# Norms by column group between products, earlier first weights, and another place for a convolution

## The chip, the cores and the metric

One core of a Trainium2 chip. The metric is the device time of one execution in microseconds, the median of the runs shown. Matrix products run on TensorE (PE); VectorE (DVE), ScalarE (ACT) and GpSimd (POOL) do the elementwise work; SyncE (SP) issues most of the other transfers, ScalarE those of the weights.

## The reference

One inference step of a two-layer decoder trunk, width 1024, on 1024 prompt tokens and 64 sample tokens (8 sequences of 8). All is float32. Cut to what matters here:

```python
def rmsnorm(x, g):
    y = x * lax.rsqrt(jnp.mean(x * x, axis=-1, keepdims=True) + NORM_EPS)
    return y * g

# layer 0: short gated convolution and RWKV-7 recurrence side by side
z = rmsnorm(x, norm_mix[0]) @ w_in0
x = x + concat(short_conv(z[:, :1536]), rwkv7(z[:, 1536:])) @ w_out0
x = x + swiglu(rmsnorm(x, norm_ffn[0]), w_gate[0], w_up[0], w_down[0])
# layer 1: forgetting attention (with a paged cache) and Mamba-2 side by side
z = rmsnorm(x, norm_mix[1]) @ w_in1
x = x + concat(attention(...), mamba2(...)) @ w_out1
x = x + swiglu(rmsnorm(x, norm_ffn[1]), ...)
y = rmsnorm(x, norm_final)
```

The FFN's hidden width is 2816. Beside y the step returns new convolution, shift, recurrence and cache rows.

## The kernel before

Activations lie transposed: 1024 features in eight tiles of 128 partitions, tokens along the columns. The 1088 tokens are worked on in two halves. H0 has 576 columns (64 sample, 512 prompt), taken as groups of 320 and 256 columns; H1 has the other 512 prompt columns, taken as one group. In the last layer's output projection and FFN the halves are cut anew: F0 has 512 columns, F1 576.

Each float32 product is three products of two rounded parts (`mm3`, L203 to L206): high by high, low by high, high by low. A weight tile of 128 output features is eight such triples for each column group, 24 matmuls, into one PSUM bank (four banks are named `acc`). `load_w` (L192) fetches the tile in 512 KB on ScalarE's queue, ScalarE rounds it to `wh`, and `k.low` subtracts to get `wl`: POOL, except in the third stage, where it is VectorE. The buffers of `wraw`, `wh` and `wl` are two deep, so a tile's rounding waits until the tile before the last has been used.

A norm (`rms`, L227, and `rms_split`) squares the eight tiles on ScalarE (L237), sums them on VectorE (L239), adds over partitions by matmuls with ones (L245), scales (L247) and takes the power -1/2 on POOL (L224), broadcasts the result over the partitions by matmuls (L255), and multiplies the eight tiles on VectorE (L269); `split` (L216) rounds each on ScalarE (L218) and subtracts on VectorE and POOL in turn (L219). All columns of a half go through each step together, and the products that follow need all of it.

The order of work is the order in which Python generators are stepped. `weave(dense, side, rate)` steps the side chain `rate` times for each step of the dense one; `beside(gen, other)` steps both in turn; `drain` runs one to its end. Each engine runs its own instructions in that order.

Layer 0: norm of H0; projection of H0 for the recurrence, with the norm of H1 woven in; then the first recurrence (of H0) beside H0's short convolution, H1's projection and three steps of H1's short convolution; then the recurrence of H1 beside H0's output projection and FFN (`out_ffn`), with six more steps of the convolution as `fill` in its norm. The last three steps stand beside the mixer norm of H0 for layer 1. A step of the convolution is one weight tile. The third stage runs H1's FFN, mixer norm and `dense` and then F0's projection and FFN beside attention and Mamba-2 of both halves. F1 comes last, with no side work, but for the final norm of F0 beside a part of it.

## Time and profile before

| | |
|---|---|
| median of 3 runs | 3342.81 us (3340.84 to 3344.05) |
| the profiled execution | 3342.04 us, span 3340.3 us |
| mean granted TensorE clock | 0.974 |
| busy share of the span | PE 95%, DVE 57%, ACT 32%, POOL 25% |

A matmul's duration in the trace is longer than the distance between two of them, since they overlap; the distance between starts is what a product costs in a row of products. The granted clock has two levels; a stretch's clock is its mean.

### The profile page before, as it was taken

Reading aid. Unit: us, or ns where it says so; the run is one execution under the profiler, and the core shown is the slowest. Engines: PE = TensorE matmul, PEld = TensorE weight load, DVE = VectorE, ACT = ScalarE, POOL = GpSimd, SP = SyncE. Lnnn points to the kernel's source line nnn. Section 1 sums busy time; section 2 is a strip of 40 time slices with the busy share of each in tenths; the row PEclk is TensorE's granted clock in tenths of the full one; section 3 lists DMA queues with packets and bytes.
Section 4 is the critical chain, followed back from the end, with each engine's and each line's share of the span. In section 5 each row is a group of like instructions: output and inputs, shape, how many; then the busy total and the mean of one; then the engine's idle time right before and its main releaser. Section 6 shows DMA issues by size and latency. Waiting matters only on the chain. (4 is left out here: it accounts for less than half of the span.)

```text
span 3340.3 us, 63263 instructions
## 1 busy us (share of the span) xinstructions
PE 3169.4 (95%) x25213; PEld 2666.9 (80%) x25213; DVE 1906.4 (57%) x3643; ACT 1058.7 (32%) x2083; POOL 834.7 (25%) x561
## 2 busy tenths in 40 slices
...
GB/s 178 116 59 79 87 96 118 73 59 56 51 66 83 83 108 148 191 151 135 108 135 163 199 154 213 240 221 175 172 171 138 113 110 135 87 105 81 83 83 78
DMA packets 238471, 409.20 MB, mean 123 GB/s; under 512 B 37632, under 2 KB 129664, under 8 KB 238176
## 3 DMA queue, kind: packets, MB, share of 16 engines
...
## 5 line engine op out<-in xcount | busy, mean ns | idle before, releaser
L204 PE MATMUL acc<-hh,wh 128*128 128x320 f32 (+2 forms) x3720 | 1264.9, 341 | 17.6 <-ACT hh L218 14.7
L206 PE MATMUL acc<-hh,wl 128*128 128x320 f32 (+2 forms) x3720 | 1255.4, 338 | 7.4 <-POOL wl L198 6.5
L205 PE MATMUL acc<-hl,wh 128*128 128x320 f32 (+2 forms) x3720 | 1254.8, 338 | 7.2 <-DVE hl L219 5.4
L204 PEld LDWEIGHTS acc<-hh,wh 128*128 128x128 f32 x3720 | 712.3, 192 | 97.5 <-ACT hh L218 19.4
L198 POOL TENSOR_TENSOR wl<-wraw,wh 128x1024 fp32r<-128x1024 f32 x225 | 539.6, 2398 | 1000.6 <-ACT wh L196 924.7
L196 ACT CAST wh<-wraw 128x1024 fp32r<-128x1024 f32 (+1 forms) x398 | 416.0, 1045 | 1139.4 <-PE acc L205 1054.1
L206 PEld LDWEIGHTS acc<-hh,wl 128*128 128x128 f32 x3720 | 712.8, 192 | 74.7 <-issue 11.1
L205 PEld LDWEIGHTS acc<-hl,wh 128*128 128x128 f32 x3720 | 713.0, 192 | 72.1 <-DVE hl L219 9.1
L205 PE MATMUL acc<-hidl,wh 128*128 128x320 f32 (+2 forms) x1056 | 353.1, 335 | 0.6 <-DVE hidl L219 0.6
L893 DVE TENSOR_TENSOR x<-x,acc 128x320 f32<-128x320 f32 (+2 forms) x528 | 270.3, 527 | 139.1 <-PE acc L206 136.1
L206 PE MATMUL acc<-hidh,wl 128*128 128x320 f32 (+2 forms) x1056 | 349.5, 332 | 0.0
L204 PE MATMUL acc<-hidh,wh 128*128 128x320 f32 (+2 forms) x1056 | 348.9, 337 | 0.4 <-ACT hidh L218 0.4
L198 DVE TENSOR_TENSOR wl<-wraw,wh 128x1024 fp32r<-128x1024 f32 x173 | 210.9, 1219 | 145.3 <-ACT wh L196 143.2
L1297 POOL DMA_INDIRECT kv<-in_cv,vidx x64 | 75.5, 1180 | 628.8 <-DVE kt L1249 134.4
L204 PEld LDWEIGHTS acc<-hidh,wh 128*128 128x128 f32 x1056 | 198.7, 189 | 24.0 <-issue 4.2
L205 PEld LDWEIGHTS acc<-hidl,wh 128*128 128x128 f32 x1056 | 199.2, 189 | 19.1 <-issue 2.2
L206 PEld LDWEIGHTS acc<-hidh,wl 128*128 128x128 f32 x1056 | 199.5, 189 | 15.6 <-issue 1.4
L219 DVE TENSOR_TENSOR hidl<-ft,hidh 128x512 fp32r<-128x512 f32 (+2 forms) x148 | 178.7, 1207 | 55.9 <-ACT hidh L218 55.8
L881 DVE SCALAR_TENSOR_TENSOR ft<-ft,acc 128x320 f32<-128x320 f32 (+2 forms) x132 | 70.1, 531 | 213.1 <-PE acc L206 212.9
L875 DVE SCALAR_TENSOR_TENSOR ft<-ft,acc 128x320 f32<-128x320 f32 (+2 forms) x132 | 69.7, 528 | 177.0 <-ACT ft L874 176.8
L218 ACT CAST hidh<-ft 128x512 fp32r<-128x512 f32 (+2 forms) x148 | 75.1, 507 | 117.5 <-DVE ft L881 114.3
L1249 DVE STREAM_TRANSPOSE kt<-kv 128x1024 f32<-128x1024 f32 x64 | 79.3, 1239 | 33.8 <-DMA kv<-in_ck 29.9
...
## 6 DMA issues: line engine op xcount, KB each, us to landing
wraw<-in_wi ACTq DMA_DIRECT2D x100, 512.0 KB
...
kv<-in_ck SPq DMA_DIRECT2D x512, 64.0 KB
...
```

Of the source, the lines that this page charges most:

```text
L196: nc.scalar.copy(wh, raw)
L198: k.low.tensor_sub(wl, raw, wh)
L204: mm(acc, wh, xh, start=first, stop=False)
L205: mm(acc, wh, xl, start=False, stop=False)
L206: mm(acc, wl, xh, start=False, stop=last)
L218: k.nc.scalar.copy(hh, v)
L219: (eng or k.nc.vector).tensor_sub(hl, v, hh)
L875: nc.vector.scalar_tensor_tensor(s[:, a:b], s[:, a:b], 1.0, pc, op0=ALU.add, op1=ALU.mult)
L881: nc.vector.scalar_tensor_tensor(s[:, a:b], s[:, a:b], 0.5, pu, op0=ALU.mult, op1=ALU.mult)
L893: nc.vector.tensor_add(xs[n][:, a:b], xs[n][:, a:b], acc[:, :b - a])
L1249: V.transpose(kt, kr)
L1297: nc.gpsimd.indirect_dma_start(out=v, out_offset=None, in_=A["cv"].rearrange("o (s r) c -> (o s) (r c)", r=2), in_offset=bass.IndirectOffs ...
```

## The change

`rms_split` becomes a class `Norm`. `group(a, b)` makes the norm of one column group; `pair` makes group 0, then the first weight tile times group 0 (below p0g0), then the norm of group 1, then the other three products of the first two weight tiles (p1g0, p0g1, p1g1). It is used before the first projection of H0, all four FFNs, and both `dense`; the norm of H1 in layer 0 is one group of 512 columns. H1 and F0 get `two`, halves of 256 columns, where a norm needs two groups. Inside `rms` the power and the broadcasts are now in one step.

In `out_ffn` the last two output tiles are made for group 0 and then for group 1, and the last down products of an FFN go by group, with both weight tiles loaded ahead. All twelve steps of H1's short convolution are now in `first()`, and the rate there is 4.2. At the start the first two weights are fetched before x, which comes in two column groups; part of the constants is loaded by `ready()`, inside the norm of H1.

```diff
 QY = 2
 VY = 3
-
-CF = (3, 6)
 
 
 class Half:
...
         self.g0 = segs[0][1] * (NS + HP) + segs[0][2]
 
...
@@ -237,7 +242,7 @@
         nc.scalar.activation(sq, x[:, lo:hi], AF.Square)
         if i:
             nc.vector.tensor_add(ss, ss, sq)
-        if i % 2:
+        if i % 4 == 3:
             yield
     pt = k.bank(tag)
     nb = len(blocks)
@@ -246,31 +251,43 @@
     r = k.bp.tile([P, 16], F32, name="rs", tag="rs", bufs=2)
     nc.vector.tensor_scalar(r[:, 8:8 + nb], pt[:, :nb], 1.0 / width, EPS, op0=ALU.mult, op1=ALU.add)
     rsqrt(k, r[:, 0:nb], r[:, 8:8 + nb])
-    yield
     out = []
     for a, b in groups:
         pb = k.bank(tag)
         for j, (_, c, w) in enumerate(blocks):
             if a <= c < b:
-                nc.tensor.matmul(pb[:, c - a:c - a + w], r[:, j:j + 1].to_broadcast([P, P]), k.con("ident")[:, :w], start=True, stop=True)
+                nc.tensor.transpose(pb[:, c - a:c - a + P], r[:, j:j + 1].to_broadcast([P, P]), k.con("ident"))
         out.append((a, b, pb[:, :b - a]))
     yield
     return out
 
 
-def rms_split(k, H, xs, gname):
-
-    nc = k.nc
-    h = k.parts(H)
-    rs = yield from rms(k, H, xs, D)
-    for i in range(KT):
-        v = k.ft(H)
-        for a, b, r in rs:
-            nc.vector.scalar_tensor_tensor(v[:, a:b], xs[i][:, a:b], k.col(gname, i), r, op0=ALU.mult, op1=ALU.mult)
-        split(k, h[0][i], h[1][i], v, nc.gpsimd if i % 2 else nc.vector)
-        if i % 2:
-            yield
-    return h
+class Norm:
+
+
+    def __init__(self, k, H, xs, gname):
+        self.k, self.H, self.xs, self.gname = k, H, xs, gname
+        self.h = k.parts(H)
+
+    def group(self, a, b):
+        k, h = self.k, self.h
+        (_, _, r), = yield from rms(k, self.H, self.xs, D, [(a, b)])
+        for i in range(KT):
+            v = k.ft(self.H)[:, a:b]
+            k.nc.vector.scalar_tensor_tensor(v, self.xs[i][:, a:b], k.col(self.gname, i), r, op0=ALU.mult, op1=ALU.mult)
+            split(k, h[0][i][:, a:b], h[1][i][:, a:b], v, k.nc.gpsimd if i % 2 else k.nc.vector)
+            if i % 4 == 3:
+                yield
+
+    def pair(self, w0, w1, m0=P, m1=P):
+
+        k, h = self.k, self.h
+        (a, b), (c, d) = self.H.two
+        yield from self.group(a, b)
+        p0 = gemm_tile(k, w0, h, a, b, m0)
+        yield from self.group(c, d)
+        p1 = gemm_tile(k, w1, h, a, b, m1)
+        return [p0, gemm_tile(k, w0, h, c, d, m0)], [p1, gemm_tile(k, w1, h, c, d, m1)]
 
 
 def by8(ap):
...
@@ -853,31 +875,39 @@
         split(k, y[0][i], y[1][i], v)
         if i % 4 == 3:
             yield
-    xs = []
-    for n in range(KT):
-        w = load_w(k, A["wo%d" % l][n])
-        x = k.xt(H)
-        for a, b, h, c, g in H.pieces(0, H.W):
-            nc.sync.dma_start(x[:, a:b], k.xs[h][n][:, c:c + b - a] if l else A["xT"][n][:, g:g + b - a])
-        for a, b in H.groups:
-            nc.vector.tensor_add(x[:, a:b], x[:, a:b], gemm_tile(k, w, y, a, b))
-        xs.append(x)
-        yield
-    h = yield from beside(rms_split(k, H, xs, "nf%d" % l), fill)
+    xs, ws = [], []
+
+    for n, js in [(n, (0, 1)) for n in range(KT - 2)] + [(n, (j,)) for j in range(2) for n in (KT - 2, KT - 1)]:
+        if not js[0]:
+            ws.append(load_w(k, A["wo%d" % l][n]))
+            x = k.xt(H)
+            for a, b, h, c, g in H.pieces(0, H.W):
+                nc.sync.dma_start(x[:, a:b], k.xs[h][n][:, c:c + b - a] if l else A["xT"][n][:, g:g + b - a])
+            xs.append(x)
+        for a, b in (H.two if len(js) > 1 else H.two[js[0]:js[0] + 1]):
+            nc.vector.tensor_add(xs[n][:, a:b], xs[n][:, a:b], gemm_tile(k, ws[n], y, a, b))
+        if len(js) > 1 or n == KT - 1:
+            yield
+    nr = Norm(k, H, xs, "nf%d" % l)
+    h = nr.h
+    first = yield from nr.pair(load_w(k, A["wg%d" % l][0]), load_w(k, A["wu%d" % l][0]))
...
@@ -893,13 +923,17 @@
                     nc.vector.tensor_add(xs[n][:, a:b], xs[n][:, a:b], acc[:, :b - a])
                     yield
 
-        if last and g == NF // GH - 1:
+        if g == NF // GH - 1:
             ws = [(q, load_w(k, A["wd%d" % l][g, q])) for q in range(2)]
             done = iter(())
-            for a, b in H.groups if len(H.groups) > 1 else ((0, 256), (256, 512)):
-                yield from beside(down(ws, a, b), done)
-                drain(done)
-                done = last(xs, a, b)
+            for a, b in H.two:
+                if last:
+                    yield from beside(down(ws, a, b), done)
+                    drain(done)
+                    done = last(xs, a, b)
+                else:
+                    drain(down(ws, a, b))
+                    yield
             yield from done
...
@@ -934,19 +968,22 @@
         self.tok = [pool.tile([P, 5 - i, 128], F32, name="tok%d" % i) for i in range(2)]
         self.past()
 
-    def dense(self, H, h):
+    def dense(self, H, nr):
 
         k = self.k
         nc, A = k.nc, k.A
         q = nc.scalar if H.i else nc.sync
-        rw = self.gates(H, h)
+        first, accs = yield from nr.pair(load_w(k, A["wi1"][0]), load_w(k, A["wfd"], 512), P, 64)
+        h = nr.h
+        rw = self.gates(H, accs)
         yield
         for j, f, parts, smp, out in ((0, 0.125, k.qp, k.qd, None), (4, 1.0, k.kp, k.kd, "kT"), (8, 1.0, None, None, "vT")):
             for p in range(4):
-                w = load_w(k, A["wi1"][j + p])
+                if j + p:
...
-            for i in range(KT):
-                nc.sync.dma_start(xs[i], A["xT"][i][:, H.cols()])
-            return xs
-
-        x0 = x_in(H0)
         k.pp = cp.tile([P, NPP], F32, name="pp")
         nc.sync.dma_start(k.pp, A["pp"])
-        k.load_con(cp, 0)
-
-        def ffn0(H, fill=iter(())):
-            xs = yield from out_ffn(k, H, 0, fill)
+        raws = [fetch(k, A["wi0"][12 + i]) for i in (12, 4)]
+        x0 = [k.xt(H0) for _ in range(KT)]
+        for a, b in H0.two:
+            for i in range(KT):
...
@@ -1528,42 +1563,41 @@
                 yield
 
         with tc.tile_pool(name="m0", bufs=1) as mp, tc.tile_pool(name="mps", bufs=1, space=PSUM) as k.mps:
-            norm = rms_split(k, H0, x0, "nm0")
-            next(norm)
+            nr = Norm(k, H0, x0, "nm0")
+            h0 = nr.h
+            tiles = [list(x) for x in drain(nr.pair(*ws))]
             m = Even(k, mp)
-            h0 = drain(norm)
             h1 = []
 
             def first():
                 yield from m.short_conv(H0, h0)
...
-                h1.extend((yield from rms_split(k, H1, x_in(H1), "nm0")))
-
-            weave(m.project(H0, h0), norm1(), 1)
+                m.ready()
+                x1 = [k.xt(H1) for _ in range(KT)]
+                for i in range(KT):
+                    nc.sync.dma_start(x1[i], A["xT"][i][:, H1.cols()])
+                yield
...
+            weave(m.project(H0, h0, tiles), norm1(), 1)
             x0 = []
-            conv1 = m.short_conv(H1, h1)
-
-            def second():
-                x0.extend((yield from ffn0(H0, islice(conv1, CF[1]))))
-
             weave(first(), m.recurrence(H0), RATE[0])
-            weave(second(), m.recurrence(H1), RATE[1])
-            h0 = drain(beside(rms_split(k, H0, x0, "nm1"), conv1))
-            drain(conv1)
+            weave(keep(ffn0(H0), x0), m.recurrence(H1), RATE[1])
             m.finish()
         with tc.tile_pool(name="m1", bufs=1) as mp, tc.tile_pool(name="mps1", bufs=1, space=PSUM) as k.mps:
             m = Odd(k, mp)
-            drain(m.dense(H0, h0))
+            drain(m.dense(H0, Norm(k, H0, x0, "nm1")))
 
             x2 = []
 
             def third():
                 x1 = yield from ffn0(H1)
-                h = yield from rms_split(k, H1, x1, "nm1")
-                yield from m.dense(H1, h)
```


VectorE's queue at the FFN norm of F1, before: L863 adds an output product to x, L239 sums squares, L247 scales, L269 multiplies x's tiles.

```order
L239 TENSOR_TENSOR ft_30517<-ft_30517,ft_30534 128x576
L863 TENSOR_TENSOR x_30446<-x_30446,acc_30449 128x320
L863 TENSOR_TENSOR x_30446<-x_30446,acc_30475 128x256
L239 TENSOR_TENSOR ft_30517<-ft_30517,ft_30537 128x576
L247 TENSOR_SCALAR rs_30546<-acc_30540 128x5
L269 SCALAR_TENSOR_TENSOR ft_30556<-x_30019,pp_220,acc_30549 128x320
L269 SCALAR_TENSOR_TENSOR ft_30556<-x_30019,pp_220,acc_30553 128x256
L269 SCALAR_TENSOR_TENSOR ft_30561<-x_30080,pp_220,acc_30549 128x320
L269 SCALAR_TENSOR_TENSOR ft_30561<-x_30080,pp_220,acc_30553 128x256
L219 TENSOR_TENSOR hl_30509<-ft_30556,hh_30501 128x576
```

After (the lines are now L888, L244, L252 and L277; `ft_31576` sums group 0, `ft_31667` group 1):

```order
L244 TENSOR_TENSOR ft_31576<-ft_31576,ft_31596 128x320
L888 TENSOR_TENSOR x_31432<-x_31432,acc_31496 128x256
L888 TENSOR_TENSOR x_31467<-x_31467,acc_31522 128x256
L252 TENSOR_SCALAR rs_31603<-acc_31599 128x3
L277 SCALAR_TENSOR_TENSOR ft_31610<-x_31066,pp_204,acc_31606 128x320
...
L224 TENSOR_TENSOR hl_31562<-ft_31634,hh_31554 128x320
L244 TENSOR_TENSOR ft_31667<-ft_31667,ft_31669 128x256
...
L244 TENSOR_TENSOR ft_31667<-ft_31667,ft_31687 128x256
L252 TENSOR_SCALAR rs_31693<-acc_31690 128x2
L277 SCALAR_TENSOR_TENSOR ft_31699<-x_31066,pp_204,acc_31696 128x256
```

The sums of group 0 stand ahead of the last adds of group 1, its scale (128x3) directly behind them, and the sums of group 1 behind all of group 0's multiplications and low parts.

TensorE's queue at the norm of H1 in layer 0, before: `acc_784` is the bank of the sums, `acc_862` that of the broadcasts, the others are tiles of the projection of H0.

```order
L206 MATMUL acc_754<-hh_237,wl_719 128x256
L245 MATMUL acc_784<-con0_222,ft_481 128x1 x4
L204 MATMUL acc_799<-hh_230,wh_795 128x320
...
L206 MATMUL acc_799<-hh_237,wl_797 128x320
L204 MATMUL acc_832<-hh_230,wh_795 128x256
...
L206 MATMUL acc_832<-hh_237,wl_797 128x256
L255 MATMUL acc_862<-con0_222,rs_789 128x128 x4
L204 MATMUL acc_874<-hh_230,wh_870 128x320
```

After (L250 makes the sums, L259 the broadcasts, L562 and L563 are small products for the recurrence):

```order
L211 MATMUL acc_743<-hh_257,wl_708 128x256
L562 MATMUL rk_1593<-la_1585,lora0_534 128x256
L563 MATMUL rk_1593<-la_1585,lora2_536 128x256
L562 MATMUL rk_1607<-la_1599,lora0_534 128x256
L563 MATMUL rk_1607<-la_1599,lora2_536 128x256
L250 MATMUL acc_773<-con0_226,ft_610 128x1 x4
L259 MATMUL acc_781<-con0_226,rs_778 128x128 x4
L209 MATMUL acc_793<-hh_250,wh_789 128x320
```

The 48 products between sums and broadcasts are gone from there. POOL's queue at the same place after the change (`rs_778` is this norm's power, `wl_791` belongs to the tile that follows it on TensorE, `wl_877` to the one after that):

```order
L203 TENSOR_TENSOR wl_791<-wraw_787,wh_789 128x1024
L203 TENSOR_TENSOR wl_877<-wraw_873,wh_875 128x1024
L229 TENSOR_TENSOR rs_778<-rs_778,con0_226 128x4
L638 TENSOR_TENSOR krz0_552<-xr_1587,eP_1641 64x4x64
L638 TENSOR_TENSOR krz1_553<-xr_1587,eP_1641 64x4x64
```

The power stands behind both subtractions.

TensorE's queue at the FFN norm of H0, before: `ch` names chunks of H1's recurrence, `acc_8348` and `acc_8436` are tiles of H1's convolution, `acc_8915` is the FFN's first.

```order
L245 MATMUL acc_8332<-con0_222,ft_7806 128x1 x5
L204 MATMUL acc_8348<-hh_465,wh_8343 128x512
...
L744 MATMUL ch_8310<-ys_8315,full_7975 64x64 x2
L204 MATMUL acc_8348<-hh_468,wh_8343 128x512
...
L721 MATMUL ch_8396<-vu_7978,big_7937 64x64
L255 MATMUL acc_8418<-con0_222,rs_8338 128x64
...
L744 MATMUL ch_8374<-ys_8379,full_7975 64x64 x2
...
L204 MATMUL acc_8436<-hh_465,wh_8432 128x512
...
L732 MATMUL ch_8374<-vu_7978,st_7977 64x64 x2
...
L206 MATMUL acc_8436<-hh_472,wl_8434 128x512
...
L204 MATMUL acc_8915<-hh_7790,wh_8911 128x320
```

After (L250, L259; L744 to L767 are the recurrence's L721 to L744 of before; `acc_8667` is p0g0):

```order
L744 MATMUL ch_8132<-vu_7683,big_7642 64x64
L250 MATMUL acc_8377<-con0_226,ft_8195 128x1 x3
L819 MATMUL ch_8058<-big_7642,vu_7683 64x64
...
L745 MATMUL ch_8132<-S_8125,krz0_552 64x64
...
L745 MATMUL ch_8132<-S_8125,krz1_553 64x64
L259 MATMUL acc_8384<-con0_226,rs_8381 128x128 x3
L767 MATMUL ch_8132<-ys_8137,full_7680 64x64 x2
...
L209 MATMUL acc_8667<-hh_8167,wh_8185 128x320
L755 MATMUL ch_8132<-vu_7683,st_7682 64x64 x2
...
L767 MATMUL ch_8154<-ys_8159,full_7680 64x64 x2
...
L755 MATMUL ch_8154<-vu_7683,st_7682 64x64 x2
...
L767 MATMUL ch_8215<-ys_8220,full_7680 64x64 x2
```

The tiles of the convolution are gone from there; between sums, broadcasts and p0g0 stand only steps of the recurrence.

## Rows read from the trace of the kernel before

**Rows 1.** The first part of the page: busy time of each engine in us, its share of the span, and its instructions.

```profile
PE 3169.4 (95%) x25213; PEld 2666.9 (80%) x25213; DVE 1906.4 (57%) x3643; ACT 1058.7 (32%) x2083; POOL 834.7 (25%) x561
```

**Rows 2.** TensorE's groups of instructions by line, of the whole run: line, engine, operation, output from inputs, shapes and count; busy us and mean ns of one; the idle time of TensorE just before them in us, and what ended it. The sums of squares (L245) and the broadcasts (L255).

```profile
L245 PE MATMUL acc<-con,ft 128*128 128x1 f32 x90 | 14.6, 283 | 34.1 <-DVE ft L239 34.1
L255 PE MATMUL acc<-con,rs 128*128 128x128 f32 (+1 forms) x90 | 19.0, 372 | 12.1 <-POOL rs L224 12.1
```

**Rows 3.** Stretches of the run. Columns: start and end in us, length, busy us (and instructions) of PE, PEld, DVE, ACT and POOL, then the granted TensorE clock as a share of full speed, the share of the DMA engines, GB/s. In order: the start; norm of H1 in layer 0; the first recurrence; the FFN norm of H0 in layer 0; the mixer norm of H0 in layer 1; the FFN norm and the mixer norm of H1; the FFN norms of F0 and of F1 in layer 1; the FFN of F1 up to its last tile; the end.

```profile
0.00:30.00 30.00, 8.50 (x32) 7.41 (x33) 16.12 (x27) 12.40 (x18) 11.02 (x20) 1.00 0.71 232
62.00:92.00 30.00, 27.06 (x191) 26.53 (x190) 21.98 (x51) 13.37 (x29) 17.50 (x14) 0.95 0.40 127
145.00:526.00 381.00, 358.75 (x4721) 274.34 (x4721) 234.64 (x627) 120.25 (x323) 122.70 (x109) 0.96 0.30 87
657.00:715.00 58.00, 53.47 (x661) 41.05 (x658) 39.25 (x93) 19.86 (x46) 21.31 (x17) 0.93 0.19 59
1258.00:1292.00 34.00, 25.51 (x153) 22.07 (x152) 29.77 (x45) 12.43 (x19) 16.53 (x12) 0.85 0.41 118
1512.00:1546.00 34.00, 30.06 (x173) 22.50 (x172) 24.08 (x55) 18.96 (x45) 6.57 (x5) 0.90 0.34 105
2028.00:2058.00 30.00, 22.22 (x135) 15.15 (x133) 21.55 (x29) 12.79 (x20) 9.95 (x9) 0.83 0.49 144
2283.00:2312.00 29.00, 25.81 (x179) 15.17 (x181) 14.90 (x21) 8.09 (x12) 13.74 (x11) 0.88 0.60 182
2880.00:2911.00 31.00, 23.87 (x143) 22.54 (x142) 18.67 (x32) 12.56 (x20) 11.86 (x8) 0.78 0.12 38
2925.00:3300.00 375.00, 375.00 (x2803) 373.66 (x2802) 163.57 (x283) 89.03 (x134) 140.58 (x60) 1.00 0.26 88
3316.00:3340.00 24.00, 10.33 (x74) 9.55 (x72) 15.82 (x42) 5.14 (x12) 1.65 (x2) 0.75 0.31 100
```

**Rows 4.** TensorE's timeline in two places where nothing waits: first and last of nine products of 256 columns, and first and last of nine products of 512 columns. Columns: start in us, duration in us, engine, line, operation, output from inputs, shape, count.

```profile
2880.23 0.28 PE L204 MATMUL acc<-hh,wh 128*128 128x256 f32 x1
2881.19 0.28 PE L206 MATMUL acc<-hh,wl 128*128 128x256 f32 x1
...
1899.83 0.39 PE L204 MATMUL acc<-hh,wh 128*128 128x512 f32 x1
1901.69 0.39 PE L206 MATMUL acc<-hh,wl 128*128 128x512 f32 x1
```

**Rows 5.** The FFN norm of F1, timelines of TensorE, VectorE, ScalarE and POOL, columns as above, with the idle time of the engine before the instruction and what ended it in brackets; then VectorE's scaling of the columns (L269) from 2881 to 2911, as count, shortest, median and longest ns; then the stretch in which the norm's first two weight tiles run, columns as in rows 3.

```profile
2885.58 2.29 PE L245 MATMUL acc<-con,ft 128*128 128x1 f32 x10 [4.11 <-DVE ft L239]
2889.37 2.50 PE L255 MATMUL acc<-con,rs 128*128 128x64 f32 x10 [1.50 <-POOL rs L224]
2893.15 0.85 PE L204 MATMUL acc<-hh,wh 128*128 128x320 f32 x2 [1.28 <-ACT hh L218]
2881.51 0.42 DVE L863 TENSOR_TENSOR x<-x,acc 128x256 f32<-128x256 f32 x1 [1.92 <-PE acc L206]
2883.05 2.47 DVE L239 TENSOR_TENSOR ft<-ft 128x576 f32<-128x576 f32 x1 [1.13 <-ACT ft L237]
2893.16 0.75 DVE L219 TENSOR_TENSOR hl<-ft,hh 128x576 fp32r<-128x576 f32 x1
2881.39 1.04 ACT L196 CAST wh<-wraw 128x1024 fp32r<-128x1024 f32 x1 [4.77 <-PE acc L205]
2892.43 0.67 ACT L218 CAST hh<-ft 128x576 fp32r<-128x576 f32 x1 [9.41 <-DVE ft L269]
2882.57 2.34 POOL L198 TENSOR_TENSOR wl<-wraw,wh 128x1024 fp32r<-128x1024 f32 x1 [3.99 <-ACT wh L196]
2888.15 1.17 POOL L224 TENSOR_TENSOR rs<-rs,con 128x5 f32<-128x5 f32 x1 [3.24 <-DVE rs L247]
L269 DVE SCALAR_TENSOR_TENSOR ft<-x,pp,acc x16: 467/506/548, 2891.1 to 2899.9; 128x320 f32<-128x320 f32 x8, 128x256 f32<-128x256 f32 x8
2893.00:2909.50 16.50, 16.10 (x100) 15.36 (x101) 13.05 (x23) 9.01 (x16) 8.12 (x5) 0.85 0.00 0
```

**Rows 6.** The start: timelines of POOL, VectorE and TensorE, and the stretch of the first two weight tiles, columns as in rows 3.

```profile
12.17 4.69 POOL L198 TENSOR_TENSOR wl<-wraw,wh 128x1024 fp32r<-128x1024 f32 x2 [8.77 <-DMA con<-in_cc]
12.27 4.69 DVE L311 TENSOR_SCALAR dv<-pp 128x4 f32<-128x4 f32 x4
26.18 0.85 PE L204 MATMUL acc<-hh,wh 128*128 128x320 f32 x2 [1.34 <-ACT hh L218]
26.00:41.50 15.50, 15.20 (x96) 14.49 (x97) 12.96 (x27) 8.44 (x15) 8.13 (x5) 1.00 0.53 158
```

**Rows 7.** The norm of H1 in layer 0, beside the projection of H0: timelines of TensorE and POOL.

```profile
68.33 0.39 PE L204 MATMUL acc<-hh,wh 128*128 128x256 f32 x1 [0.78 <-DVE rs L247]
87.65 0.42 PE L206 MATMUL acc<-hh,wl 128*128 128x320 f32 x1 [2.16 <-POOL wl L198]
69.41 2.40 POOL L198 TENSOR_TENSOR wl<-wraw,wh 128x1024 fp32r<-128x1024 f32 x1
```

**Rows 8.** The FFN norm of H0 in layer 0, beside the recurrence of H1: TensorE's timeline. L732 is one step of the recurrence's chunk, at two successive chunks; L205 is a low-part product of a weight tile.

```profile
675.74 0.34 PE L732 MATMUL ch<-vu,st 128*64 128x64 f32 x4
680.03 0.34 PE L732 MATMUL ch<-vu,st 128*64 128x64 f32 x4
687.61 0.41 PE L205 MATMUL acc<-hl,wh 128*128 128x320 f32 x1 [2.77 <-DVE hl L219]
```

80 lines of the change are left out of this document (49 added, 31 removed).

## The prediction

> **What bounds the kernel now.** I read the page's first part, then the waits of TensorE by line, then a table of stretches, then timelines at the stretches that lose most. TensorE is busy 95% of a span of 3340.3 us [rows 1], so only its idle time and its half clock can be won. The sums of squares (L245) wait 34.1 us in all for VectorE, and the broadcasts (L255) 12.1 us for the power on POOL [rows 2]: norms are where it waits. I call *loss* of a stretch its length less busy time times granted clock, that is, what is lacking to full-speed work. From [rows 3]: start 30 - 8.50 x 1.00 = 21.5; norm of H1 (62 to 92) 30 - 27.06 x 0.95 = 4.3; first recurrence 381 - 358.75 x 0.96 = 36.6; FFN norm of H0 (657 to 715) 58 - 53.47 x 0.93 = 8.3; mixer norm of H0 (1258) 34 - 25.51 x 0.85 = 12.3; FFN norm of H1 (1512) 34 - 30.06 x 0.90 = 6.9; mixer norm of H1 (2028) 30 - 22.22 x 0.83 = 11.6; FFN norms of F0 (2283) and F1 (2880) 29 - 25.81 x 0.88 = 6.3 and 31 - 23.87 x 0.78 = 12.4; the end 24 - 10.33 x 0.75 = 16.3. Between 2925 and 3300 nothing is lost.
>
> **The FFN norm of F1, step by step** (nothing else is there to run). The last output product issues at 2881.19 [rows 4]. Its add comes at 2881.51; the last square stands behind a weight cast of 1.04 us and the last sum (2.47 us, begun at 2883.05 while POOL runs a weight subtraction from 2882.57 to 2884.91) ends at 2885.52. TensorE idles 4.11, 1.50 and 1.28 us before sums, broadcasts and first product at 2893.15, 11.9 us after that last product [rows 5]. Two weight tiles (96 matmuls) are through at about 2909.5 [rows 5]: 28.3 us for 12.8 us of work.
> After the change, group 0's last adds, squares and sums run beside the 48 products of 256 columns of group 1: 48 x 0.12 = 5.8 us of cover (0.12 us is (2881.19 - 2880.23)/8 [rows 4]). What stays bare for group 0 is the last add 0.42, scale 0.17, power 1.17, broadcasts and waits about 1, one product on VectorE 0.55, one cast 0.67: about 3.9 us. So the first product comes 8 us earlier. Then VectorE paces: 8 x 0.51 for group 0 and 4 x 0.42 for its low parts (0.75 at 576 columns [rows 5], by columns) are 5.8, near 6 us, while 24 matmuls of 320 columns would need 24 x 0.12 x 320/256 = 3.6. VectorE's queue has all of group 0 ahead of group 1's seven adds (7 x 0.42 = 2.9, by the add of 256 columns at 2881.51). Then sums, scale, power, broadcast and first column product again, 3.9 us less what overlaps. TensorE has p1g0 behind group 1's broadcast, so it stands from about 10.4 to 14.3 us. The three remaining tiles end at about 23.5 us; the half clock after the two idle stretches adds 1.7 to 3.4. Gain about 3 us, bounds 5 gained and 2 lost.
>
> **The other norms, by the same account.**
> - Start. POOL's two weight subtractions (4.69 us) hold VectorE's four small products for the same 4.69 us; the first product is at 26.18 and 96 matmuls are through at 41.5 [rows 6]. The change has x in two parts and the weights ahead, but now both weight casts (1.04 each, as in [rows 5]) stand ahead of seven of group 0's squares on ScalarE, and the subtractions again block the sums. First product about 20, p1g0 about 31, both tiles at about 39 to 41. Taken: 2 gained (7 gained to 2 lost).
> - Norm of H1. Before, 48 products lie between the sums and the broadcasts; after, none. POOL has the power behind a 2.40 us subtraction [rows 7], which waits for a 1.04 us cast, which waits for the buffer of the tile just ended: 1.04 + 2.40 + 1.17 is 4.6, less what small products cover, and some half clock, against the 0.78 and 2.16 us there now [rows 7]. Taken: 3 lost (0 to 5).
> - Mixer norm of H0. The cover of 3 convolution steps is gone, but the same column order helps: 2 gained (5 gained to 3 lost). FFN norm of F0: 3 gained (6 to 0).
> - FFN and mixer norms of H1: attention beside them fills either way, and VectorE's extra instructions (two of 256 columns for one of 512) eat the head start: nothing (3 either way).
> - Final norm of F0: sums and broadcasts now adjoin in a stretch that lost nothing [rows 3]; a power and its waits, 1.5 us lost (0 to 2). The end has the same chain as before: nothing.
>
> **The convolution of H1.** Nine of its steps (24 matmuls of 512 columns at (1901.69 - 1899.83)/8 = 0.2325, 5.6 us each [rows 4]) move to the first recurrence, 50 us of cover. There each step of the dense side now carries 4.2 steps of recurrence and not 5.5. If the loss of 36.6 goes with that ratio, 36.6 x (1 - 4.2/5.5) = 8.6, say 9 gained (0 to 15). It is paid for at the FFN norm of H0, where six of the steps were. The recurrence of H1 still runs there: its step L732 recurs after 680.03 - 675.74 = 4.29 us even with cover [rows 8]. Before, two convolution tiles (11.2 us) stand between the sums and the first product; after, four such steps, 3 x 4.29 = 12.9 us, have beside them 3.6 us of p0g0 and at most 5.1 of their own products (three steps of five groups of four, 0.34 each). 4.2 to 9.3 us are bare, against the one gap of 2.77 [rows 8], so 1.4 to 6.5 more; with the second chain of the norm and the half clock I take 6 lost (2 to 12).
>
> **Column halves.** 600 products of 512 columns become 1200 of 256: 600 x (0.24 - 0.2325) = 4.5 us lost. Loads of both down weights ahead, and the constants woven into the projection of H0, cost nothing: the weights' queue runs beside 24 or more products, and SP is not waited for there. Bare, a weight's cast and subtraction are 1.04 + 2.40 us; twice that in a whole run would be the bound.
>
> **Sum.** -2 + 3 - 9 + 6 - 2 + 0 + 0 - 3 - 3 + 1.5 + 4.5 = -4.0. The profiled execution took 3342.04 (span 3340.3 and 1.7 around it), so 3338.0; the median shown is 0.77 above it: 3338.8, rounded 3339. A measurement of this kernel can tell 0.2%, 6.7 us, from no change: faster is below 3336.1, slower above 3349.5.
>
> **Rivals.**
> - *The head start is kept.* First products come earlier by 8 us at F1, 6 at the start, about 4 each at the mixer norm of H0 and at F0. If group 1's chain hides behind p0g0, those count in full: 22 in place of the 10 in my sum, so 12 better: 3327. For it: TensorE would have 3.6 to 6 us to run in that time, and the power is only 1.17. Against it: group 1's seven sums stand behind group 0's last low part on VectorE.
> - *The clock stays low.* In the stretch in which F1's two tiles run now, the granted clock is 0.85: it comes back during VectorE's paced product [rows 5]. After the change each of six norms has two idle stretches with a paced product between. If the clock is at its lower level (1.2 GHz) through p0g0 and p1g0, p0g0 takes 7.2 and not 6, p1g0 7.2 and not 3.6: 4.8 a site; today's loss of 2.5 (16.5 x 0.15) off, 2.3 x 6 = 14, less some 2.5 a norm at F1 and the start already counted: +9, 3348. The Trainium skill has this as a rule (TensorE: Matmul & The Clock Gate, section "A second HAM failure mode: psum-queue depth-cycling"): frequent short idling between groups of matmuls makes the gate swing between its two levels. The rows of the kernel before show the lower level after long waits; a short wait such as 2.16 us near 85 us left 62 to 92 at 0.95.
> - *The lost cover decides: slower.* Place: FFN and mixer norms of H0. If the recurrence of H1 is bare there, 12 lost rather than 6 in the first; the mixer norm, left with no side work, loses 3 rather than gaining 2; the first recurrence gives 4 rather than 9, since it waits for chains that a nearby tile covers already. 6 + 5 + 5 = 16 worse: 3355. It decides from where those three reach 11 of the 16. For it: [rows 8], and that the tiles of the norm are the smallest cover there is. Against it: the loss in the first recurrence, 36.6, is over four times that at this norm.
> - *Nothing of it works as meant* needs no price of its own: it is the last case without its gain.
>
> **Numbers.** Forecast (3331 to 3347) 0.40, head start 0.26, low clock 0.13, lost cover 0.21. Faster: 0.24 of the second and 0.16 of the first, 0.40. Slower: 0.20 of the last, 0.05 of the third, 0.01: 0.26. Within: 0.34. Range 3318 to 3355: it takes in both outer cases nearly whole; the forecast's own is 3331 to 3347.
>
> **What would show it.** Right: at F1 the wait before the first sums is under 0.5 us and a second one of 3 to 4 us stands before group 1's; the norm of H1 waits over 3 us for POOL; 145 to about 575 has a loss under 32; the FFN norm of H0 loses 12 to 16. Wrong, if the second waits are under 1 us (head start), if clocks of the norm stretches fall below those of before (low clock), or if the first recurrence loses as much as before (lost cover).

## The result: 32 us slower

| | before | changed |
|---|---|---|
| median (4 runs each) | 3342.57 us | 3374.53 us |
| lowest to highest | 3340.84 to 3344.05 | 3371.17 to 3379.39 |
| profiled execution's span | 3340.3 us | 3369.4 us |

The ratio is 1.0097, interval 1.0079 to 1.0114. The first part of the page of the changed kernel answers to [rows 1]; the line of its sums (L250) among TensorE's groups and what the broadcasts (L259) waited for answer to [rows 2].

```profile
PE 3184.8 (95%) x25783; PEld 2715.9 (81%) x25783; DVE 1904.8 (57%) x3788; ACT 1081.5 (32%) x2200; POOL 843.4 (25%) x598
...
L250 PE MATMUL acc<-con,ft 128*128 128x1 f32 x90 | 14.9, 276 | 33.3 <-DVE ft L244 33.1
```

```profile
  POOL rs L229: 21.2, 17
```

TensorE is 15.4 us longer busy at a lower mean clock (0.969 for 0.974). The sums wait as long as before (34.1 us then), and the broadcasts wait 9 us more (12.1 then): the norms have more chains now, and no less waiting.

Stretches of the changed kernel, columns as in [rows 3]: the start, the norm of H1, first recurrence, FFN norm of H0, mixer norm of H0, FFN norm of F1 and its first part.

```profile
0.00:30.00 30.00, 9.03 (x34) 7.68 (x35) 16.32 (x33) 13.79 (x29) 12.21 (x22) 0.98 0.66 205
62.00:92.00 30.00, 27.76 (x187) 27.53 (x188) 25.09 (x58) 15.34 (x33) 14.53 (x11) 0.89 0.36 111
145.00:565.00 420.00, 393.61 (x4875) 302.04 (x4875) 242.53 (x630) 125.41 (x323) 137.45 (x115) 0.96 0.28 84
679.00:715.00 36.00, 31.10 (x318) 24.03 (x316) 23.58 (x64) 13.27 (x38) 14.90 (x16) 0.76 0.14 45
1281.00:1315.00 34.00, 25.49 (x157) 22.97 (x156) 21.42 (x43) 14.76 (x32) 16.46 (x14) 0.85 0.42 129
2902.00:2933.00 31.00, 22.57 (x128) 20.82 (x127) 22.34 (x44) 16.81 (x37) 15.07 (x13) 0.78 0.10 34
2902.00:2921.00 19.00, 12.10 (x58) 10.68 (x58) 12.03 (x26) 8.29 (x19) 9.74 (x8) 0.71 0.16 56
```

Length less busy times clock gives 42.1 us for the first recurrence (36.6 before), 12.4 for the FFN norm of H0 (8.3), 12.3 for the mixer norm (12.3), and 13.4 where F1's norm lost 12.4. For the first recurrence that comparison says little: the stretch of before was shorter, and in the same 420 us the kernel before loses 46.9.

```profile
145.00:565.00 420.00, 392.74 (x5190) 302.27 (x5190) 260.97 (x687) 133.92 (x353) 134.26 (x116) 0.95 0.30 89
```

In a stretch of 420 us the rounding of the clock alone is 2 us either way, and a stretch cannot be the same one in two kernels with different work in it. So I also lay the traces against each other at equal work: the time at which TensorE has done the same amount of weight-tile products (each counted at its full-speed distance to the next), and, in the recurrences, the same chunk less the tiles that changed place. The delay against the kernel before, in us (columns e1 to e12 are the runs described below):

| place (its time before) | changed | e1 | e3 | e7 | e8 | e9 | e12 | e10 | e11 |
|---|---|---|---|---|---|---|---|---|---|
| end of H0's first projection (127) | 8.6 | 2.5 | 0.7 | -3.4 | 2.5 | -9.5 | -8.8 | -9.3 | 8.9 |
| first chunk of H1's recurrence (564) | 13.3 | 14.6 | 11.8 | 2.8 | 8.6 | -0.2 | -10.2 | -6.8 | 9.1 |
| its third unit (669) | 24.5 | 37.3 | 24.5 | 16.0 | 17.1 | 8.9 | -2.9 | -6.8 | 24.5 |
| its last chunk (945) | 15.9 | 24.7 | 16.9 | 6.7 | 5.5 | -6.7 | -19.3 | -9.3 | 15.3 |
| after the mixer norm of H0 (1402) | 23.6 | 36.6 | 29.1 | 14.4 | 6.1 | 0.7 | -11.3 | -9.0 | 23.7 |
| after the mixer norm of H1 (2118) | 11.7 | 37.9 | 31.6 | 8.1 | -0.5 | -2.2 | -17.2 | -14.6 | 12.2 |
| before F1's norm (2832) | 16.8 | 40.0 | 33.6 | 16.8 | -17.2 | -2.8 | -15.0 | -16.3 | 14.4 |
| in F1's FFN (3001) | 21.7 | 40.5 | 35.3 | 18.8 | 9.2 | -5.2 | -17.0 | -18.7 | 15.1 |
| last product (3333) | 29.1 | 42.1 | 41.0 | 26.4 | 18.1 | 2.5 | -9.3 | -10.9 | 22.8 |

How fine this is shows in e1: its code up to the first row is that of before, and it stands 2.5 us behind; in one trace, less than 3 us is not read. In the first recurrence even that is too fine: the changed kernel and e7 to e9 have the same code there and lose 4.7, 6.2, 6.1 and 9.3 between the first two rows. Each column is one execution, and the traces come from several chips, on which the kernel before has medians from 3333.56 to 3342.57; so the delay at the end of a trace and the ratio can differ by several us. Products of column halves count as work, 6.1 us more for the 624 products that were split than for whole ones; their extra cost so appears only in the last row, and rows 2118 to 3001 of the kernels with halves look that much better.

**Start.** TensorE of the changed kernel, columns as in [rows 5], as in the timelines that follow:

```profile
15.75 1.44 PE L250 MATMUL acc<-con,ft 128*128 128x1 f32 x6 [15.75 <-DVE ft L244]
18.38 0.90 PE L259 MATMUL acc<-con,rs 128*128 128x128 f32 x3 [1.19 <-POOL rs L229]
20.41 0.64 PE L209 MATMUL acc<-hh,wh 128*128 128x320 f32 x1 [1.13 <-ACT hh L223]
29.81 1.01 PE L250 MATMUL acc<-con,ft 128*128 128x1 f32 x4 [2.37 <-DVE ft L244]
31.86 0.69 PE L259 MATMUL acc<-con,rs 128*128 128x128 f32 x2 [1.04 <-POOL rs L229]
```

The first product comes at 20.41 and not 26.18 [rows 6]. But group 1's sums come at 29.81, after a second wait, and the two tiles end 1.6 us later than before.

**Norm of H1.** TensorE, VectorE, ScalarE and POOL:

```profile
62.79 1.51 PE L250 MATMUL acc<-con,ft 128*128 128x1 f32 x8 [4.01 <-DVE ft L244]
65.64 1.12 PE L259 MATMUL acc<-con,rs 128*128 128x128 f32 x4 [1.34 <-POOL rs L229]
59.55 2.30 DVE L405 SCALAR_TENSOR_TENSOR ft<-o_shift,pp,ft 128x1 f32<-128x1 f32 x1
61.96 0.68 DVE L244 TENSOR_TENSOR ft<-ft 128x512 f32<-128x512 f32 x1
58.03 0.21 DVE L405 SCALAR_TENSOR_TENSOR ft<-o_shift,pp,ft 128x1 f32<-128x1 f32 x1
58.29 1.03 ACT L201 CAST wh<-wraw 128x1024 fp32r<-128x1024 f32 x1
59.45 2.39 POOL L203 TENSOR_TENSOR wl<-wraw,wh 128x1024 fp32r<-128x1024 f32 x1 [5.34 <-ACT wh L201]
64.58 1.01 POOL L229 TENSOR_TENSOR rs<-rs,con 128x4 f32<-128x4 f32 x1 [2.75 <-DVE rs L252]
```

The sums in the kernel before:

```profile
62.97 0.95 PE L245 MATMUL acc<-con,ft 128*128 128x1 f32 x8
```

The wait is there, but it stands before the sums and not for POOL's power, as forecast: POOL is free for 2.75 us before the power starts. The last sum (61.96) stands behind an instruction of one column that takes 2.30 us and ends when POOL's weight subtraction does (59.45 + 2.39 = 61.84). In the kernel before, the last sum ends at 60.40 (59.71 + 0.69), and TensorE is busy until then and beyond with the 48 products of a weight tile, the last issued at 62.85, so its sums (62.97) wait for nothing; in the changed kernel the sums stand ahead of that tile, and the 48 products between sums and broadcasts are gone as well.

**FFN norm of F1.** TensorE and VectorE:

```profile
2903.25 0.28 PE L211 MATMUL acc<-hh,wl 128*128 128x256 f32 x1
2903.37 0.73 PE L250 MATMUL acc<-con,ft 128*128 128x1 f32 x6
2905.29 0.54 PE L259 MATMUL acc<-con,rs 128*128 128x128 f32 x3 [1.19 <-POOL rs L229]
2906.96 0.63 PE L209 MATMUL acc<-hh,wh 128*128 128x320 f32 x1 [1.13 <-ACT hh L223]
2916.98 1.02 PE L250 MATMUL acc<-con,ft 128*128 128x1 f32 x4 [2.32 <-DVE ft L244]
2919.36 0.61 PE L209 MATMUL acc<-hh,wh 128*128 128x320 f32 x1
2933.16 0.41 PE L211 MATMUL acc<-hh,wl 128*128 128x320 f32 x1 [1.70 <-POOL wl L203]
2942.96 0.65 PE L259 MATMUL acc<-con,rs 128*128 128x128 f32 x4 [1.34 <-POOL rs L229]
2912.82 0.41 DVE L244 TENSOR_TENSOR ft<-ft 128x256 f32<-128x256 f32 x1
2913.39 3.53 DVE L244 TENSOR_TENSOR ft<-ft 128x256 f32<-128x256 f32 x6 [0.16 <-ACT ft L242]
```

Here group 0 does as forecast: no wait before its sums, first product 3.71 us after the last output product (11.9 before, [rows 5]). Then group 1's seven sums begin on VectorE only at 2912.82, and its first product comes 16.1 us after that last one. The third weight's low part then waits 1.70 us for POOL, since the pair holds both weight buffers to its end. Laid against each other at equal work within this stretch, the two traces put the norm and its two tiles level (0.4 us gained between 2860 and 2911 of before); 2.8 us go with the third weight (2911 to 2915) and 4.3 at the final norm of F0 (2919 to 2925), where e7, with the old final norms, loses 0.1; some 2 us come back around them. With all sums first (e8, e9, e10, e12) the norm and its two tiles gain 5.7 to 6.4.

**A place the prediction did not look at.** At the second FFN group of H0, TensorE and VectorE, and in the last line TensorE's wait for the same chain in the kernel before:

```profile
1004.40 0.42 PE L209 MATMUL acc<-hidh,wh 128*128 128x320 f32 x1 [1.70 <-DVE x L923]
1007.66 0.39 PE L209 MATMUL acc<-hidh,wh 128*128 128x256 f32 x1 [2.11 <-DVE x L923]
1002.34 1.68 DVE L1127 COPY pl<-plf 128x512 f32<-128x512 f32 x1 [2.53 <-DMA plf<-in_clf,pidx]
1003.93 0.41 DVE L923 TENSOR_TENSOR x<-x,acc 128x256 f32<-128x256 f32 x1
1004.93 2.29 DVE L1131 TENSOR_TENSOR_SCAN plf<-prs,pl 128x1024 f32<-128x1024 f32 x1
...
1284.02 0.39 PE L1101 MATMUL rk<-ptot,con 128*128 128x8 f32 x2 [2.35 <-DVE ptot L1099]
```

`plf` is the third stage's gather through the page table. Its buffers come free when layer 0's pool (`m0`) is done; since no convolution step remains for the mixer norm, that is earlier, and the copies and the scan, which ran from 1277 on in the kernel before, now stand in the middle of the FFN's adds (L923). VectorE waits 2.53 us for the transfer, and TensorE waits 1.70 and 2.11 us for the adds behind it. With the half clock after it the delay rises by 6.1 us here.

### The profile page after: what moved, and what is told of

It is laid out like the page before. It is cut to its first block, busy times and chain, and to the rows that moved or that the text cites. A ratio compares the mean times of both kernels' runs of the same rounds, so it can differ in the third digit from the quotient of the medians.

```text
span 3369.4 us, 64778 instructions
## 1 busy us (share of the span) xinstructions
PE 3184.8 (95%) x25783; PEld 2715.9 (81%) x25783; DVE 1904.8 (57%) x3788; ACT 1081.5 (32%) x2200; POOL 843.4 (25%) x598
## 5 line engine op out<-in xcount | busy, mean ns | idle before, releaser
L209 PE MATMUL acc<-hh,wh 128*128 128x256 f32 (+4 forms) x3896 | 1300.2, 334 | 15.9 <-ACT hh L223 9.7
L211 PE MATMUL acc<-hh,wl 128*128 128x256 f32 (+4 forms) x3896 | 1286.3, 330 | 10.8 <-POOL wl L203 9.6
L210 PE MATMUL acc<-hl,wh 128*128 128x256 f32 (+4 forms) x3896 | 1290.4, 332 | 5.6 <-DVE hl L224 3.5
L209 PEld LDWEIGHTS acc<-hh,wh 128*128 128x128 f32 (+1 forms) x3896 | 750.6, 193 | 91.3 <-issue 15.5
L211 PEld LDWEIGHTS acc<-hh,wl 128*128 128x128 f32 (+1 forms) x3896 | 751.1, 193 | 66.7 <-POOL wl L203 12.6
L210 PEld LDWEIGHTS acc<-hl,wh 128*128 128x128 f32 (+1 forms) x3896 | 751.3, 193 | 63.8 <-DVE hl L224 7.7
L201 ACT CAST wh<-wraw 128x1024 fp32r<-128x1024 f32 x398 | 415.8, 1045 | 1093.0 <-PE acc L210 981.6
L209 PE MATMUL acc<-hidh,wh 128*128 128x320 f32 (+2 forms) x1088 | 357.5, 335 | 4.8 <-DVE x L923 3.8
L923 DVE TENSOR_TENSOR x<-x,acc 128x320 f32<-128x320 f32 (+2 forms) x544 | 271.8, 517 | 136.9 <-PE acc L211 135.6
L203 DVE TENSOR_TENSOR wl<-wraw,wh 128x1024 fp32r<-128x1024 f32 (+1 forms) x171 | 208.3, 1218 | 143.5 <-ACT wh L201 134.7
L211 PEld LDWEIGHTS acc<-hidh,wl 128*128 128x128 f32 x1088 | 208.0, 191 | 15.1 <-issue 2.1
L223 ACT CAST hh<-ft 128x256 fp32r<-128x256 f32 (+3 forms) x152 | 71.1, 478 | 95.5 <-DVE ft L277 62.4
```

Of the source, the lines that this page charges most:

```text
L201: nc.scalar.copy(wh, raw)
L203: k.low.tensor_sub(wl, raw, wh)
L209: mm(acc, wh, xh, start=first, stop=False)
L210: mm(acc, wh, xl, start=False, stop=False)
L211: mm(acc, wl, xh, start=False, stop=last)
L223: k.nc.scalar.copy(hh, v)
```

## The experiments

Ratios are to the kernel before on the same chip (medians there 3333.56 for e1 to e4, 3337.61 for e5 to e8, 3337.25 for e9 to e11, 3340.51 for e12). The ratios carry the verdicts, the traces the places.

### e1 to e4: parts of the change, alone

**e1**: the kernel before with the convolution's new place and rate, and nothing else.

```diff
-RATE = (5.5, 6, 1.8, 1.8, 1)
+RATE = (4.2, 6, 1.8, 1.8, 1)
...
-                yield from islice(conv1, CF[0])
+                yield from m.short_conv(H1, h1)
...
-            weave(second(), m.recurrence(H1), RATE[1])
+            weave(keep(ffn0(H0), x0), m.recurrence(H1), RATE[1])
```

> The kernel before with the convolution of H1 moved alone (all twelve steps beside the first recurrence, rate 4.2; norms and start as before). Theory A (several separate costs): the first recurrence loses about 5 us more, the page-table chain of the attention's past moves up into the FFN of H0 and stalls TensorE about 6 us near 970 to 1000 where the kernel before has no wait, and the mixer norm of H0 stands bare, about 4 us more: 15 above before, 3357 (3351 to 3363). Theory B (lost cover decides nearly all of the 32 us): 3367 or more. Theory C (the convolution is harmless, the norms do it): 3340 to 3346.

3377.46, ratio 1.0128 (1.0113 to 1.0142): alone it costs more than the whole change, and the time lies where the rival of lost cover had it, not at the 3357 that was expected. The table's column e1 gives the places: 12 in the first recurrence, where the prediction had a gain, a peak of 23 more at the FFN norm of H0 of which 10 stay, and 12 from there to the end of the mixer norm. TensorE at a wait of the recurrence on the way to the peak, at the page table's place and at the mixer norm (L706 is a recurrence step, L283 the sums of the mixer norm):

```profile
607.04 0.65 PE L706 MATMUL rk<-t,nt 32*32 32x32 f32 x32 [3.06 <-DVE t L723]
1013.33 0.41 PE L209 MATMUL acc<-hidh,wh 128*128 128x320 f32 x1 [1.69 <-DVE x L1041]
1016.61 0.58 PE L209 MATMUL acc<-hidh,wh 128*128 128x256 f32 x1 [2.13 <-DVE x L1041]
1299.07 1.23 PE L283 MATMUL acc<-con,ft 128*128 128x1 f32 x5 [6.39 <-DVE ft L277]
```

The page table's two waits are there to 0.02 us, so they come with the convolution's move and not with the norms.

**e2**: the kernel before with the start and the norm of H1 of the changed one.

```diff
-            norm = rms_split(k, H0, x0, "nm0")
...
+            tiles = [list(x) for x in drain(nr.pair(*ws))]
...
+                nr = Norm(k, H1, x1, "nm0")
+                yield from nr.group(0, 512)
```

> The kernel before with the changed start and norm of H1 alone (weights first, x in two column groups, constants inside the norm of H1, first two weight tiles by column group). Theory A: the traces of before and after stand 8.6 us apart at the end of H0's projection and this is carried to the end: 3351 (3347 to 3354). Theory B: lost cover is all, so the start costs nothing: 3340 to 3345.

3349.51, ratio 1.0052 (1.0038 to 1.0065). In the trace it is 1.1 us behind before the norm of H1 and 8.7 behind it, as the changed kernel is, and 9.1 at the end. By the ratio it costs 17 us: the kernel before is 8.5 us faster on this chip than in the trace that I compare with. Where the other 8 lie is not shown.

**e3**: e1, and all four FFNs by column group, with `out_ffn` as in the changed kernel; its core:

```diff
-    h = yield from beside(rms_split(k, H, xs, "nf%d" % l), fill)
+    nr = Norm(k, H, xs, "nf%d" % l)
+    h = nr.h
+    first = yield from nr.pair(load_w(k, A["wg%d" % l][0]), load_w(k, A["wu%d" % l][0]))
```

> The kernel before with the convolution moved and the four FFNs by column group; start and both mixer norms as before. Theory A: the run of the convolution alone, plus 3 at F1 and its next weights and plus 2 for the final norm of F0, less some 5 at the FFN norms of H1: within 4 us of the run of the convolution alone. Theory C (column groups cost): 10 us or more above it.

3380.82, ratio 1.0140 (1.0125 to 1.0154), the same as e1 within the intervals. At the FFN norm of H0 the groups do win back 8 to 13 us of what the convolution's leaving costs (24.5 against 37.3 at the third unit), and the rest of the run gives it back, 5.7 us of it by the column halves at the distances of the table.

**e4**: the changed kernel with the page table's transfer held back until the FFN of H0 is done.

```diff
-    def past(self):
+    def past(self, late):
...
+            V.tensor_copy(idx, late[:, 0:1])
...
-            m = Odd(k, mp)
+            m = Odd(k, mp, x0[7])
```

> The changed kernel, but the page-table chain may start only when the last column of x of H0's FFN is final (its index tile is first written from x). Theory A: the 1.70 and 2.11 us that TensorE waits near 1003 to 1008 and the half clock behind them go, 6 us in all, of which some 2 come back at the mixer norm of H0, where the kernel before had 2.35: 3370 to 3372 against 3374.5. Rival: the waits there are of the two held down weights, so 3374 or more.

3372.99, ratio 1.0128 (1.0110 to 1.0145). The two waits near 1004 are gone, and a wait of the same chain stands at the mixer norm, where nothing covers it:

```profile
1297.04 0.57 PE L1256 MATMUL rk<-ptot,con 128*128 128x8 f32 x2 [4.97 <-DVE ptot L1254]
```

Between 1255 and 1300 of before this kernel falls 5.5 us behind, where the changed one loses nothing. Moved, not removed; and the 3 us that were expected are not in the ratio, which is no better than that of the changed kernel.

### e5 and e6: which steps of the convolution

**e5** has 6, 6 and 0 steps in the three places (before: 3, 6, 3; changed: 12, 0, 0), **e6** 9, 0 and 3 (at the rate 4.6), both on the kernel before.

```diff
-RATE = (5.5, 6, 1.8, 1.8, 1)
+RATE = (5.0, 6, 1.8, 1.8, 1)
...
-                yield from islice(conv1, CF[0])
+                yield from islice(conv1, 6)
```

> The kernel before with six steps of the convolution beside the first recurrence (rate 5.0), six in the FFN norm of H0 as before, and none left for the mixer norm of H0. Theory A (three prices, read from the run with all twelve steps moved: first recurrence +5 to +13 for nine steps, FFN norm of H0 +10, mixer norm with the page-table chain moved up +12): 3 to 5 for three more steps in the recurrence and 12 for the mixer norm and the chain: +16 (+12 to +20). Rival (the price is that of the FFN norm alone): +5 or less.

> The kernel before with nine steps of the convolution beside the first recurrence (rate 4.6), none in the FFN norm of H0 and three at the mixer norm of H0 as before. Theory A: 4 to 8 in the recurrence, 10 at the FFN norm, and the page-table chain stays late, where its cover is: +16 (+12 to +22), and together with the run of 6, 6 and 0 about the price of all twelve. Rival (the price is the mixer norm and the chain alone): +8 or less.

3364.50, ratio 1.0073 (1.0055 to 1.0090), and 3362.26, ratio 1.0068 (1.0052 to 1.0084). Both cost more than the 16 us expected of each (24 and 23 by the ratios). They part the costs. In the first recurrence e5 loses 14.2 us (from -0.3 to 13.9) with 3 more steps, e6 6.3 (-1.0 to 5.3) with 6 more. Between 564 and 945, e6, whose FFN norm is bare, falls from 5.3 to 31.0 and comes back to 16.7; e5, which kept it covered, goes from 13.9 to 8.7. Between 945 and 1402, e5, whose mixer norm is bare, loses 11.5, with the page table's two waits (1.71 and 2.12 us at 997 and 1001); e6 loses 1.1.

### e7 and e8: the norms of the changed kernel

**e7** puts the norm of H1, the final norms and the norm in Mamba-2 back into their old steps.

```diff
-                nr = Norm(k, H1, x1, "nm0")
-                yield from nr.group(0, 512)
-                h1.extend(nr.h)
+                h1.extend((yield from rms_split(k, H1, x1, "nm0")))
```

> The changed kernel, with the norm of H1 in layer 0, the final norms and the norm in Mamba-2 made in the old steps (a step between power and broadcasts, so that two column tiles of products stand between). Theory A: the 4.0 and 1.3 us of idle time near 58 to 66 and the half clock behind them go, 7 us, and 3 to 4 at the final norm of F0: 1.000 above before instead of 1.0097 less 0.0033, that is a ratio near 1.0065. Rival (the start alone, not this norm, costs the 8.6): 1.009 or more.

3369.09, ratio 1.0090 (1.0070 to 1.0109). The norm of H1 is 12 us better (-3.4 for 8.6 at 127), and 9 of it last to 1402; by 2832 the two are level, at 16.8. A lead in layer 0 was eaten in the third stage, so the ratio, 1.0065 expected, moved by less than its interval; the rival, that the start alone costs the 8.6 us, is not borne out by the trace.

**e8** makes the squares and sums of both groups before group 0 is scaled, with one step of the generator for a group's sums and not two.

```diff
-        yield from self.group(a, b)
+        s0 = self.sums(a, b)
+        yield
+        s1 = self.sums(c, d)
+        yield
+        yield from self.group(a, b, s0)
         p0 = gemm_tile(k, w0, h, a, b, m0)
-        yield from self.group(c, d)
+        yield from self.group(c, d, s1)
```

> The changed kernel, with the squares and sums of both column groups ahead of group 0's multiplications, so that group 1's sums no longer stand behind them on VectorE. If that queue order is what gives the head start back: the second idle stretch at F1 (2.32 and 1.03 us before sums and broadcasts, and the low clock behind it) goes, 3 to 5 us at each of F1, F0 and the mixer norm of H0, 1 to 3 elsewhere: a ratio near 1.006. Rival (the second stretch is short beside the paced products and the held weights): 1.009 or more, and new waits of group 0 instead.

3358.02, ratio 1.0062 (1.0048 to 1.0076). TensorE at the start (L337 sums, L343 broadcasts; no wait of 1 us follows until 34), and before F1's output projection:

```profile
15.61 1.44 PE L337 MATMUL acc<-con,nsum 128*128 128x1 f32 x6 [15.61 <-DVE nsum L328]
18.36 0.90 PE L343 MATMUL acc<-con,rs 128*128 128x128 f32 x3 [1.31 <-POOL rs L229]
20.39 0.64 PE L209 MATMUL acc<-hh,wh 128*128 128x320 f32 x1 [1.13 <-ACT hh L223]
...
2850.33 1.12 PE L209 MATMUL acc<-hh,wh 128*128 128x320 f32 x3 [6.64 <-ACT hh L223]
```

The second chain is hidden: 4.8 us ahead at 55 where the changed kernel was 1.0 behind. But each norm also steps its neighbour less often, so some side work was left over for the end of the third stage, and its chain is bare there, 6.64 us in one wait: 17 us ahead at 2832, 9 behind at 3001. e9, which has the old number of steps, has no such fall.

### e9 to e12: the repairs together, and the rate

**e9**: e7 and e8 in one, with as many generator steps as in the changed kernel (a `yield` after every fourth square, and `yield from self.sums` for both groups).

> The changed kernel with two repairs together: the sums of both groups of a norm are made before group 0 is scaled (with as many steps of the generator as the changed kernel has, 10), and the norm of H1 and the final norms are back in their old steps. If the losses found so far are those of the norms by group and add up, this takes 9 us at the norm of H1 and 12 to 18 us in the pairs off the changed kernel and the stall before F1 does not come: ratio to the kernel before 1.000 to 1.003. If the convolution's new place (6 to 14 us lost in the first recurrence and about 6 us for the page table's chain) decides, it stays at 1.005 or more.

3340.88, ratio 1.0017 (1.0005 to 1.0030). 27 us of the 32 go with these two repairs (1.0097 - 1.0017 = 0.0080). Alone they took off 2 and 12 (e7 and e8), so they do not simply add up: e9 also has the steps that e8 left out.

**e10**: the start, the FFN and mixer norm of H1, F0 and F1 as in e9; for H0's FFN and mixer norms, the norm of H1 and the convolution, the code of before.

```diff
-            xs = yield from out_ffn(k, H, 0)
+            xs = yield from (out_ffn(k, H, 0) if H.i else out_ffn_old(k, H, 0, fill))
...
+            h0 = drain(beside(rms_split(k, H0, x0, "nm1"), conv1))
...
-            drain(m.dense(H0, Norm(k, H0, x0, "nm1")))
+            drain(m.dense0(H0, h0))
```

> The kernel before with its convolution where it was (3, 6 and 3 steps), H0's FFN and mixer norms and the norm of H1 as they were, and column groups (sums of both first) only where no convolution stood: the start, the FFN and mixer norms of H1, F0 and F1. If the convolution's move is what the change lost by, this is faster than the kernel before: 5 us at the start, about 4 at F1, 0 to 8 between, less some 4 for the column halves: ratio 0.995 to 0.999. If column groups lose by themselves (half clock, second chains), 1.001 or more.

3329.46, ratio 0.9977 (0.9968 to 0.9986): faster than both kernels, than the one before by 0.23%.

**e11** and **e12**: the changed kernel, and e9, with the first recurrence's rate as before.

```diff
-RATE = (4.2, 6, 1.8, 1.8, 1)
+RATE = (5.5, 6, 1.8, 1.8, 1)
```

> The changed kernel with the rate of the first recurrence as before, 5.5 and not 4.2: the recurrence ends about 70 us before the dense side, and the last convolution tiles run with nothing beside them. If waits come with each step of the recurrence, whatever lies beside it, the loss between 145 and 575 is the same 42 us and the time moves less than 3 us. If the loss falls with the number of recurrence steps beside one weight tile, as the prediction had it, the stretch loses 5 to 10 us more than the changed kernel; if tiles without side work recover what the prediction promised, 5 to 10 us less.

> The kernel of run e9 (sums of both groups first, norm of H1 and final norms in their old steps, all twelve convolution steps in the first recurrence) with the rate 5.5 and not 4.2. Run e9 fell 9 us behind between the first and the fifth unit of the first recurrence, and run e11 (rate 5.5) kept its distance to the kernel before there. If the lower rate makes that loss, this one holds its lead of 9 us to the end of the first recurrence, and if nothing later eats it the ratio is 0.998 to 1.000; what is left against run e10 is then the page table's chain, 6 to 7 us. If the loss belongs to the twelve convolution tiles, or comes back at the FFN norm of H0 as in run e11, it is 1.001 to 1.003 as in run e9.

e11: 3363.28, ratio 1.0077 (1.0063 to 1.0091), whose interval meets that of the changed kernel, so its time decides between none of the cases expected. In the first recurrence it holds its delay (8.9 to 9.1), where the changed kernel goes from 8.6 to 13.3; at the third unit of H1 both stand at 24.5, for a reason that I did not find. e12: 3333.02, ratio 0.9981 (0.9968 to 0.9994), 12 us better than e9 by one number. The first recurrence in e9, e11 and e12, columns as in [rows 3]:

```profile
145.00:565.00 420.00, 393.55 (x4832) 300.75 (x4832) 236.24 (x625) 126.62 (x326) 136.08 (x112) 0.95 0.28 87
```

```profile
145.00:565.00 420.00, 397.03 (x4889) 305.44 (x4888) 246.72 (x641) 124.38 (x323) 139.55 (x116) 0.96 0.28 88
```

```profile
145.00:565.00 420.00, 397.96 (x4879) 305.03 (x4879) 243.35 (x637) 130.58 (x334) 139.69 (x113) 0.97 0.30 92
```

Losses of 46.1, 38.9 and 34.0. What the old rate does can be read from the order of the products. The last chunk of the first recurrence comes at 437.8 in the kernel before and at 446.8 in e11, 9.0 later, as its start is. Between it and the first chunk of H1's recurrence lie 360 products of 512 columns in e11 and e12, 144 in the kernel before: the difference is 216, all nine moved tiles (192 at the rate 4.2). So at 5.5 the recurrence runs as it did and the moved tiles run behind its last chunk; at 4.2 most of them are spread along it, and there they cost time.

e12 also has the page table's waits (1.71 and 2.11 us), which is most of what it gives back before 1402. With the rate of before and the sums first, e12 can't be told from e10, which has the convolution's old place and H0's old FFN and mixer norms.

## Why the prediction was wrong

It forecast 3339, up to 3355, and the time was 3374.5. By its own terms, against the changed kernel's delay between the rows of the table (they add up to 29.1 = 3369.4 - 3340.3):

| term | forecast | measured |
|---|---|---|
| start | -2 | +1.0 |
| norm of H1 | +3 | +7.6 |
| convolution: first recurrence | -9 | +4.7 |
| convolution: FFN norm of H0 | +6 | +2.6 (peak +11.2) |
| mixer norm of H0, and before it from 945 | -2 | +7.7, 6.1 of it the page table |
| norms of H1 | 0 | -11.9 (-6.1 without the count of the halves) |
| F0 and the rest to 2832 | -3 | +5.1 |
| F1, final norm of F0 | -3 + 1.5 | +4.9 |
| column halves, end | +4.5 | +7.4, 6.1 of it the halves by the count |

- **"If the loss of 36.6 goes with that ratio"** is the step that failed worst: 9 us of gain that is a loss. It took the recurrence's losses as lack of cover, which tiles spread along it would fill. The runs show that they don't fall with the rate: with 5.5, where the tiles stand behind the recurrence, the loss against before stays the same to 0.2 us (e11) or falls by 1.4 (e12), and at every other rate, where they stand along it, the same stretch loses 5 to 14 (changed, e1, e3, e5 to e9). That 5.0 lost 14.2 and 4.6 only 6.3 is one trace each, with other numbers of tiles moved, and no more than a hint that the rate's size is not what counts. Why tiles along the recurrence cost time is not shown.
- **Norm of H1**: the place and sign were right, the wait was not. "POOL has the power behind a subtraction" was right of the queue, but the subtraction was done 2.74 us before the power began (61.84 and 64.58), and the power cost 1.34 us. The wait of 4.01 stands before the sums: VectorE's last sum was held up during that subtraction, and the weight tile that covered this place before now comes after it. The half clock is the rest (0.89 in 62 to 92, 0.95 before). e7 removes it all.
- **FFN norm of H0**: that six steps of cover were lost was right. The size, taken from [rows 8], held neither way: e1 and e3 show 23 and 13 us at the peak and 10 and 5 at the end, probably because H1's recurrence, once late, then runs beside more products; no run shows that reason.
- **A step moved past a queue was missed.** The convolution's last steps held the pool that the page table's buffers follow. Not one term speaks of it; it costs 6 to 7 us in the changed kernel, e1, e5, e9, e11 and e12 and does not appear in e6 and e10, which keep the last three steps at the mixer norm.
- **F1 and the start**: "VectorE's queue has all of group 0 ahead of group 1's seven adds" was right, and so was the head start of group 0 (3.71 us, forecast 3.9). "From about 10.4 to 14.3" was 16.1. So the norm itself came out level and not 3 us ahead; the loss of 4.9 is the third weight's (2.8, a wait of 1.70 in it) and the final norm's (4.3 with the clock behind its 1.34, for 1.5 forecast), less the 2 around them. e8 and e12 confirm the reason by taking it away: with all sums first, the second wait is gone at the start (e8) and 0.34 us at F1 (e12).
- **Column halves**: 624 products were split and not 600, which at the prediction's distances is 4.7 us; the 6.1 is the table's count. No run takes the halves away alone, so their price is an estimate either way.
- **Norms of H1** were put at nothing. Nearly 6 us of the 11.9 are the halves, which the table counts as work here and as time only in its last row. Without that count the stretch moves by 1.2, -1.6 and -0.9 us in e9, e10 and e12, nothing as forecast, and by -6.1 in the changed kernel, which is lost again by 2832, as side work that was only put off would be.

Of the rivals, the lost cover had the direction right and the sizes wrong: 2.6 us at the FFN norm (12 by it), 1.6 at the mixer norm beside the page table (3), and 4.7 lost in the first recurrence, for which it still took a gain of 4. Its step of 16 from the forecast to 3355 is less than half of the 35.5 that came; the page table, the norm of H1, the start and F1 are not in it. The head start is kept only where the sums come first (e8 to e10, e12). The low clock is seen, in p0g0 as that rival had it (0.50, the lower level, from 2907 to 2913), but at F1 it is no new cost: 0.78 in 31 us, as before, and in the 19 us from the last output product on 0.71 against 0.64 before. Below before stand the norm of H1 (0.89 for 0.95) and the FFN norm of H0 (0.76 for 0.88 in 679 to 715). The Trainium skill (TensorE: Matmul & The Clock Gate, section "A second HAM failure mode: psum-queue depth-cycling") says that short idling between groups of matmuls makes the gate swing; the stretch from 2902 to 2921, with waits of 1.19, 1.13 and 2.32 us and a mean between the two levels, agrees. These are p0g0 in the changed kernel, then the 19 us before and in e12, where the second wait is hidden (0.82):

```profile
2907.00:2913.00 6.00, 4.78 (x15) 4.03 (x16) 5.66 (x11) 3.73 (x10) 3.95 (x4) 0.50 0.27 87
...
2881.00:2900.00 19.00, 12.11 (x55) 10.80 (x54) 11.69 (x22) 6.13 (x9) 7.58 (x5) 0.64 0.10 33
...
2874.00:2893.00 19.00, 15.60 (x95) 14.00 (x94) 15.32 (x32) 9.81 (x22) 13.16 (x12) 0.82 0.17 56
```
